# Small tiles of a decoder trunk padded and packed, so that the tiles behind them lie elsewhere in SBUF

## The chip, the cores and the metric

The kernel runs on one core of a Trainium2 chip. The metric is the device time of one execution in microseconds (us): the median of three runs is 1328.34 us, from 1328.08 to 1328.96. The profile is of one further execution.

## The reference

Two layers of a decoder trunk over 256 tokens of width 1024, all in float32. What matters of it here:

```python
for l in range(DEPTH):                                   # DEPTH = 2
    x = x + 0.5 * swiglu_ffn(x, ffn1_norm[l], ffn1_wi[l], ffn1_wo[l])      # 1024 -> 2 x 2816 -> 1024
    h = rms_norm(x, mix_norm[l])
    (sb_q, sb_k, sb_v, mla_cq, mla_ckv, mla_kr, nsa_q, ck, cv, sk, sv, wk, wv,
     nsa_gate, merge_gate) = jnp.split(h @ w_in[l], offsets, axis=-1)
    o_sb = stick_breaking_attention(...)                 # 8 heads of 64
    o_mla = mla_attention(...)                           # 8 heads, low-rank q and kv
    o_nsa = nsa_attention(..., nsa_gate, ...)            # 8 heads, three branches
    gates = jax.nn.sigmoid(merge_gate).reshape(B, S, 3, D_MODEL)
    y = (gates[:, :, 0] * (o_sb @ proj_sb[l]) + gates[:, :, 1] * (o_mla @ proj_mla[l])
         + gates[:, :, 2] * (o_nsa @ proj_nsa[l]))
    x = x + y @ w_out[l]
    x = x + 0.5 * swiglu_ffn(x, ffn2_norm[l], ffn2_wi[l], ffn2_wo[l])
```

## The kernel before, in words

**Products.** The tokens are two row tiles of 128 (`t` = 0, 1). Each float32 operand is split into a high part (rounded to float32r) and the low rest, and `mm3` (L528 to L532) makes three matmuls of a product: high by high (L530), high by the weights' low part (L531), low by the weights' high part (L532). The stationary operand is 128 x 128 of the activations, laid with the contracted dimension on the partitions: `hThi`, `hTlo` for the normed input, `gh`, `gl` for the inner activations of the FFN, `oh`, `ol` for the outputs of the attentions, `cT` for the latents of the MLA. The moving operand is the weights, `whi` and `wlo`, mostly 512 columns. The result goes to a PSUM bank `acc`.

**Weights.** They come from HBM in slabs of 128 x 1024 (`load_slab` in the FFNs, `weights` in the mixer): two DMAs into `raw`, then ScalarE rounds to `whi` (L514, L817) and VectorE subtracts to `wlo` (L515, L819). Four slabs are in the buffer.

**Stages of a layer.** `ffn`: first the products with `hT` in column chunks of 512 (`chunk`), where for a slab two steps of the contraction run into the same `acc` before the row tile changes; `glu` gates the result, and `flush` transposes it (L692) into `gh`, `gl`. Then `out_rows` multiplies `gT` by the 22 slabs of the output weights: for a slab it runs t = 0 and 1 and for each the column halves c = 0 and 1, three matmuls each, so that the bank changes after every three. That makes 264 matmuls in an `out_rows` of an FFN, in four of them (two layers with two FFNs). `mixer`: a planner (`Planner.run`) merges generators into one static order for TensorE, VectorE and ScalarE, by costs in a table; `t_chunk` (L849) is its loop for the products with weights, the same loop for the products with `hT` and for those of `merge` (L1147) with `oh`, `ol`. Behind the mixer `out_rows` runs the output projection with `hT`-like tiles.

**Order.** The order on TensorE, VectorE and ScalarE is fixed when the program is built. A tile's place in SBUF follows from the pools: a pool lays its tiles one behind another in each partition, and the pools stand behind each other (`cp`, `sm`, `wp`, `hp`, and then, in turn, `fp` of an FFN or `mp` of a mixer). A shift of one small tile in `hp` therefore shifts all of `fp` and `mp`.

Names that the change touches: `rn` (L572), the three scaled copies of a token's inverse norm; `krg0`, `krg1` (L875), the rotary key and gate logits of the MLA and NSA; `sg` (L1443), the gates of the NSA; `qrb` (L1022), the buffer of the query's rotation, with its one slot `s_qrb`; `new_oT` (L766, called in L1195), the tiles `oh` and `ol`; `wf` (L745), four work tiles with the slots `s_wf`.

Of the kernel before, what the change touches and what calls it, by code (L numbers as in the profile page):

```python
# [10 lines left out]
F = mybir.dt.float32  # L11
# [10 lines left out]
NT = 2  # L22
# [201 lines left out]
def event():  # L224
    return Tok(None)
# [78 lines left out]
def use_v(n, *deps, slots=()):  # L304

    return "V", 0.065 + 0.00106 * n, 0.15 + 0.00106 * n, deps, slots


def use_v1(n, *deps, slots=()):

    return "V", 0.13 + 0.00052 * n, 0.215 + 0.00052 * n, deps, slots


def use_a(n, *deps, slots=()):

    return "A", 0.085 + 0.00085 * n, 0.19 + 0.00085 * n, deps, slots
# [19 lines left out]
def use_g(us, *deps, slots=()):  # L336

    return "G", us, us, deps, slots
# [5 lines left out]
WR_BUFS = 4  # L344
TH_BUFS = 7
# [11 lines left out]
def decoder_trunk(ctx, tc, x_in, wts, gains, lcon, cst, out, depth=DEPTH):  # L357
# [7 lines left out]
    hp = ctx.enter_context(tc.tile_pool(name="hp", bufs=2))  # L365
# [10 lines left out]
    def att_tile():  # L376
        return pb.tile([128, 512], F, tag="ps", name="att")
# [156 lines left out]
    def rstd(ss, inv, w=1, p=128):  # L534
        r = sm.tile([128, 16], F, tag="rs", name="rs")
        nc.vector.tensor_scalar(ss[:p, :w], ss[:p, :w], inv, EPS, op0=OP.mult, op1=OP.add)  # L536
        nc.gpsimd.tensor_tensor(r[:p, :w], ss[:p, :w], mh[:p, :w], op=OP.pow)  # L537
        return r
# [25 lines left out]
    def norm_scale(t):  # L564

        sq = att_tile()
        ss = sm.tile([128, 16], F, tag="ss", name="ss")
        for c in range(2):
            nc.scalar.activation(sq, xs[t][:, c * 512:(c + 1) * 512], AF.Square, accum_out=ss[:, c:c + 1])
        nc.vector.tensor_scalar(ss[:, 0:1], ss[:, 0:1], ss[:, 1:2], None, op0=OP.add)  # L570
        r = rstd(ss, 1.0 / D)
        q = hp.tile([128, 3], F, tag="rn", name="rn", bufs=4)  # L572
        for i, m in enumerate((1.0, 0.5, 0.125)):
            nc.vector.tensor_scalar(q[:, i:i + 1], r[:, 0:1], m, None, op0=OP.mult)
        return q
# [28 lines left out]
    def out_rows(lhs, kts, between=None, last=False):  # L604
# [28 lines left out]
        for t in range(NT):  # L633
            cmajor = last or t == 0
            order = [(k, c) for k in tail for c in range(2)]
            if cmajor:
                order.sort(key=lambda kc: kc[1])
            for k, c in order:
                run(t, c, k, sls[k - tail[0]])
                if t == 1 and not last and c == 0 and k - tail[0] in (0, 1):  # L640
                    to_T(hT[0], hs[0], (k - tail[0],))
                if cmajor and k == kts - 1:
                    finish(t, c)
            if not cmajor:
                for c in range(2):
                    finish(t, c)
            if not last:
                rn[t] = norm_scale(t)
# [90 lines left out]
    def mixer(l):  # L739
        es = ExitStack()  # L740
        mp = es.enter_context(tc.tile_pool(name="mp", bufs=1))
        hs, hT, rn = nxt[0]
        xd = dp.tile([NT, 128, D], F, tag="xd", name="xd")

        def wf():  # L745
            return mp.tile([128, 384], F, tag="wf", name="wf", bufs=4)
# [7 lines left out]
        def tmp(n=768):  # L754
            return mp.tile([128, 768], F, tag="tmp", name="tmp", bufs=1)[:, :n]
# [10 lines left out]
        def new_oT():  # L766
            return (mp.tile([128, 4, S], R, tag="oh", name="oh", bufs=2),
                    mp.tile([128, 4, S], R, tag="ol", name="ol", bufs=2))
# [9 lines left out]
        s_bank = Slots(8)  # L778
        s_acc, s_tp, s_att = Slots(4, s_bank), Slots(2, s_bank), Slots(3, s_bank)
        s_w, s_raw = Slots(W_BUFS - len(ready)), Slots(RAW_BUFS)  # L780
        s_wf, s_wr, s_qk, s_th, s_tmp, s_qrb, s_of = Slots(4), Slots(WR_BUFS), Slots(4), Slots(TH_BUFS), Slots(1), Slots(1), Slots(1)

        def events(*n):
            return [events(*n[1:]) for _ in range(n[0])] if n else event()
# [87 lines left out]

        cT = mp.tile([128, 2, NT, 3, 128], R, tag="r3", name="cT")
        cT = cT[:, 0], cT[:, 1]
        krg = [mp.tile([128, 56], F, name=f"krg{t}") for t in range(NT)]  # L875
        ev_hT, ev_rn, ev_cT, ev_krg = events(2), [Tok(2.0), Tok(4.0)], events(NT), events(NT)

        def hT_rest():
# [93 lines left out]
        def mla_q(i):  # L972
            for t in range(NT):
                ks = []
                for c in range(2):
                    k = yield use_p(384, 6, ev_cT[t], slab_ev[i][c], slab_ev[i + 1][c], slots=(s_acc,))
                    a = acc_tile()
                    for s in range(2):
                        mm3(a[:, 0:384], cut(cT, A, t, s, A), cut(slabs[i + s][1], A, slice(c * 384, (c + 1) * 384)),
                            start=s == 0, stop=s == 1)  # L980
                    ks.append(event())
                    spawn(mla_q_out(t, c, a, k, ks[c]))
                spawn(mla_q_norm(t, ks), 0.4)
            s_w.put(k, k)
            mark()
            mark()
# [7 lines left out]
        def t_rope(dst, x, tb, t, H, d, buf, k):  # L994

            c, s = tb[0][:, t, :], tb[1][:, t, :]
            h = d // 2
            for o, i in ((0, h), (h, 0)):
                k1 = yield use_v(H * h, k)
                nc.vector.tensor_tensor(buf[:, :, o:o + h], x[:, :, i:i + h], bc(s[:, o:o + h], H), op=OP.mult)  # L1000
            k1 = yield use_v(H * d, k1)
            nc.vector.tensor_tensor(x, x, bc(c, H), op=OP.mult)
            k1 = yield use_v(H * d, k1)
            nc.vector.tensor_tensor(dst, x, buf, op=OP.add)
            return k1

        def mla_q_norm(t, ks):
            x = mq[t].rearrange("p (h d) -> p h d", h=8)
            k = yield use_a(768, *ks, slots=(s_tmp,))
            sq = tmp()  # L1010
            nc.scalar.activation(sq, mq[t], AF.Square)
            k = yield use_v(768, k)
            ss = sm.tile([128, 16], F, tag="ss", name="ss")
            nc.vector.tensor_reduce(ss[:, 0:8], sq.rearrange("p (h d) -> p h d", h=8), axis=AX.X, op=OP.add)
            s_tmp.put(k)
            k = yield use_v1(8, k)
            r = rstd(ss, 1.0 / 96, w=8)
            k = yield use_g(2.5, k)
            k = yield use_v(768, k)
            nc.vector.tensor_tensor(x, x, r[:, 0:8, None].to_broadcast([128, 8, 96]), op=OP.mult)  # L1020
            yield "-", 0.0, 0.0, (), (s_qrb,)
            b = mp.tile([128, 8, 32], F, tag="qrb", name="qrb", bufs=1)  # L1022
            k = yield from t_rope(x[:, :, 64:96], x[:, :, 64:96], tab["mq"], t, 8, 32, b, k)
            s_qrb.put(k)
            ev_mq[t].set(k)

        def mla_kv(i):
# [164 lines left out]
                yield from merge(c, *gs[c], o_nsa, ev_onsa, False, final=True)  # L1192


        o_sb, o_mla, o_nsa = new_oT(), new_oT(), new_oT()  # L1195
        ev_osb, ev_omla, ev_onsa = events(4), events(4), events(4)
        ev_sbpv, ev_sbm = event(), event()

# [241 lines left out]
                spawn(put_o(o_mla, p, oT, k, ev_omla), 0.01 * p)  # L1440


        sg = mp.tile([128, NT, 3, 8], F, name="sg")  # L1443
        ev_prep, ev_sg = events(NT), event()

        def nsa_prep():
# [381 lines left out]
```

## Time and profile before

| | |
|---|---|
| median of three runs | 1328.34 us |
| the profiled execution | 1328.05 us, its span 1326.3 us |
| TensorE (PE) busy | 1302.1 us, 98% of the span, 6623 matmuls |
| VectorE (DVE) busy | 893.9 us, 67% |
| ScalarE (ACT) busy | 796.4 us, 60% |
| share of the chain that ended last | PE 85%, ACT 7%, DVE 6%, issue 2% |
| mean granted clock of TensorE | 0.997 of 2.4 GHz |

The span is the time from the first to the last instruction; the execution is 1.75 us longer. A matmul's record is longer than the distance to the next one, since matmuls are pipelined: the pace of a stream is read from the starts of two records and the number of matmuls from the one to the other, not from a record's length. Where the text speaks of a record's length it says so.

### The profile page before, as it was taken

The numbers are of one execution on the slowest core, as the hardware profiler recorded it, in microseconds if no ns is written. First come the engines' busy times: TensorE is split into PE (matmuls) and PEld (weight loads), VectorE is DVE, ScalarE is ACT, GpSimd is POOL, SyncE is SP. The second block draws the span as 40 slices with busy tenths as digits, with TensorE's granted clock in tenths as the row PEclk, the third lists the DMA queues.
The fourth block names the chain that finished last, engine by engine and source line by source line (L and its number), as shares of the span: only waits on it lengthen the run. The fifth ranks groups of instructions, "written<-read, shape, count | busy, mean of one in ns | idle before, by whom it ended". The sixth has DMA issues, their size and how long they took to land.

```text
span 1326.3 us, 19987 instructions
## 1 busy us (share of the span) xinstructions
PE 1302.1 (98%) x6623; PEld 1078.1 (81%) x6623; DVE 893.9 (67%) x1852; ACT 796.4 (60%) x1654; POOL 43.4 (3%) x50
## 2 busy tenths in 40 slices
PE   7999999999899999999999999999989999999998
PEld 6888888888777888888888888888878778888887
DVE  6655557988997775555466554679879876755553
ACT  5545447796888555454464544478868884645442
POOL 0000000210000000000000000011100000000000
PEclk9999999999999999999999999999999999999999
DMA  7765557545434656555656565565453356565563
GB/s 226 245 190 177 189 179 219 181 127 175 128 90 135 184 174 198 189 183 183 191 179 216 178 190 181 188 217 160 133 173 110 102 159 176 173 191 183 183 189 112
DMA packets 124504, 230.77 MB, mean 174 GB/s; under 512 B 13928, under 2 KB 15600, under 8 KB 124400
## 3 DMA queue, kind: packets, MB, share of 16 engines
q1 hardware_dynamic: 124144, 228.97, 55.5%
q8 instruction: 52, 0.85, 0.3%
q0 software_dynamic: 256, 0.52, 0.1%
q14 instruction: 52, 0.43, 0.1%
HBM read 225.77 MB, written 3.15 MB: 173 GB/s over the span
## 4 chain that ended last, share of the span: by engine, by line
PE 85%; ACT 7%; DVE 6%; issue 2%; DMA 0%; SPq 0%; ACTq 0%; DVEq 0%
PE acc L530 26%; PE acc L532 26%; PE acc L531 26%; ACT wf L1340 2%; ACT whi L817 2%; PE tp L692 1%; DVE wlo L819 1%; ACT wf L1367 1%; DVE wr L1384 1%; DVE wlo L515 1%; DVE x L626 1%; PE att L1290 1%; PE att L1726 1%; PE att L1262 1%; DVE wf L1350 0%
## 5 line engine op out<-in xcount | busy, mean ns | idle before, releaser
L515 DVE TENSOR_TENSOR wlo<-raw,whi 128x512 fp32r<-128x512 f32 (+1 forms) x560 | 361.9, 687 | 318.0 <-ACT whi L514 316.6
L514 ACT ACTIVATE whi<-raw 128x512 fp32r<-128x512 f32 (+1 forms) x560 | 323.0, 623 | 374.7 <-PE acc L532 366.4
L530 PE MATMUL acc<-whi,hThi 128*128 128x512 f32 (+2 forms) x1248 | 480.3, 385 | 0.5 <-ACT hThi L525 0.5
L532 PE MATMUL acc<-whi,hTlo 128*128 128x512 f32 (+2 forms) x1248 | 470.4, 377 | 0.6 <-DVE hTlo L526 0.6
L531 PE MATMUL acc<-wlo,hThi 128*128 128x512 f32 (+2 forms) x1248 | 469.0, 376 | 0.0
L532 PEld LDWEIGHTS acc<-whi,hTlo 128*128 128x128 f32 x1248 | 235.3, 189 | 44.6 <-DVE hTlo L526 1.0
L530 PEld LDWEIGHTS acc<-whi,hThi 128*128 128x128 f32 x1248 | 235.7, 189 | 39.5 <-ACT hThi L525 1.0
L531 PEld LDWEIGHTS acc<-wlo,hThi 128*128 128x128 f32 x1248 | 235.9, 189 | 37.7
L819 DVE TENSOR_TENSOR wlo<-raw,whi 128x512 fp32r<-128x512 f32 (+1 forms) x276 | 181.4, 681 | 42.2 <-ACT whi L817 40.6
L817 ACT ACTIVATE whi<-raw 128x512 fp32r<-128x512 f32 (+1 forms) x276 | 162.9, 618 | 53.9 <-PE acc L532 42.4
L530 PE MATMUL acc<-whi,gh 128*128 128x512 f32 x352 | 140.1, 398 | 0.0
L532 PE MATMUL acc<-whi,gl 128*128 128x512 f32 x352 | 139.0, 395 | 0.0
L531 PE MATMUL acc<-wlo,gh 128*128 128x512 f32 x352 | 139.0, 395 | 0.0
L532 PEld LDWEIGHTS acc<-whi,gl 128*128 128x128 f32 x352 | 66.1, 188 | 15.9
L531 PEld LDWEIGHTS acc<-wlo,gh 128*128 128x128 f32 x352 | 66.2, 188 | 15.3
L530 PEld LDWEIGHTS acc<-whi,gh 128*128 128x128 f32 x352 | 66.1, 188 | 15.3
L537 POOL TENSOR_TENSOR rs<-ss,mh 128x1 f32<-128x1 f32 (+4 forms) x30 | 36.6, 1223 | 1034.0 <-DVE ss L536 1012.6
L1340 ACT ACTIVATE wf<-wf,mn 128x128 f32<-128x128 f32 x96 | 42.7, 446 | 12.1 <-DVE mn L1350 11.7
L530 PE MATMUL acc<-whi,oh 128*128 128x512 f32 x96 | 41.2, 429 | 0.5 <-DVE y L1155 0.5
L532 PE MATMUL acc<-whi,ol 128*128 128x512 f32 x96 | 39.1, 408 | 0.0
L531 PE MATMUL acc<-wlo,oh 128*128 128x512 f32 x96 | 39.1, 407 | 0.0
L683 DVE SCALAR_TENSOR_TENSOR g<-acc,rn,sil 128x512 f32<-128x512 f32 (+1 forms) x48 | 33.6, 703 | 2.9 <-PE acc L532 0.8
(274 smaller groups left out, 1262.6 us busy)
## 6 DMA issues: line engine op xcount, KB each, us to landing
raw<-in_wts SPq DMA_DIRECT2D x824, 256.0 KB, 2.7
gain<-in_gains SPq DMA_DIRECT2D x5, 512.0 KB, 5.7
xd<-x SPq DMA_DIRECT2D x4, 512.0 KB, 4.4
x<-xd SPq DMA_DIRECT2D x4, 512.0 KB, 4.1
raw<-in_wts SPq DMA_DIRECT2D x8, 184.0 KB, 2.5
lc<-in_lcon SPq DMA_DIRECT2D x2, 528.0 KB, 7.5
x<-in_x SPq DMA_DIRECT2D x4, 256.0 KB, 5.3
out_dram<-x SPq DMA_DIRECT2D x4, 256.0 KB, 2.0
```

Source lines behind the costliest of these rows:

```text
L514: nc.scalar.activation(hi[:, c:c + m], raw[:, :m], AF.Copy)
L515: nc.vector.tensor_tensor(lo[:, c:c + m], raw[:, :m], hi[:, c:c + m], op=OP.subtract)
L530: nc.tensor.matmul(o, a[0], b[0], start=start, stop=False)
L531: nc.tensor.matmul(o, a[0], b[1], start=False, stop=False)
L532: nc.tensor.matmul(o, a[1], b[0], start=False, stop=stop)
L537: nc.gpsimd.tensor_tensor(r[:p, :w], ss[:p, :w], mh[:p, :w], op=OP.pow)
L626: nc.vector.scalar_tensor_tensor(xv, accs[t, c], 0.5, xv, op0=OP.mult, op1=OP.add)
L683: nc.vector.scalar_tensor_tensor(g[:, :fn], b[:, :fn], rn[t][:, 0:1], s[:, :fn], op0=OP.mult, op1=OP.mult)
L692: nc.tensor.transpose(tp[:, j * 128:(j + 1) * 128], g[:, j * 128:(j + 1) * 128], ident)
L817: nc.scalar.activation(hl[0][:, c:c + m], raw[:, :m], AF.Copy)
L819: nc.vector.tensor_tensor(hl[1][:, c:c + m], raw[:, :m], hl[0][:, c:c + m], op=OP.subtract)
L1340: nc.scalar.activation(E[i][:, cs], E[i][:, cs], AF.Exp, scale=-1.0, bias=mn[:, q:q + 1], accum_out=su[:, q:q + 1])
```

## The change

The number of instructions, their order on all five engines and what they compute stay as they are (TensorE has 5930 rows in the order before and as many after, all alike but for line numbers and buffers' numbers). All semaphore waits stay too, except that two VectorE instructions wait for an earlier instruction of VectorE itself that stands three places before the one they waited for. What changes is where tiles lie. `rn` becomes 32 columns wide where it had 3; `krg0`, `krg1` and `sg` become parts of one tile `small` of 1024 bytes a partition; `qrb` goes, and the rotation takes one of the four `wf` tiles for it; and the six tiles of `new_oT` and `small` are allocated ahead of the tiles behind them.

Start of each tile in a partition, modulo 512 bytes, as the built programs have it (all slices of 128 columns and of 512 columns that the products with weights take lie whole multiples of 512 bytes further, except the second half of a slab of 440 columns, which lies 224 more):

| tile | before | after |
|---|---|---|
| `whi`, `wlo`, `raw`, `hThi`, `hTlo` | 32 | 32 |
| `gh`, `gl`, `sil`, `g` (FFN) | 160 | 32 |
| `oh`, `ol` (outputs of the attentions) | 96 | 32 |
| `cT`, `zw`, `V0`, `V1` | 160 | 32 |
| `nx0`, `nx1` | 96 | 32 |
| `Vc`, `pch`, `pcl`, `wf`, `th`, `qk`, `wr`, `of`, `tmp` | 288 | 32 |
| `rt`, `zk`, `hv` and `ident` (constants) | 352, 352 or 96, 352 or 96, 320 | unchanged |

```diff
@@ -569,7 +569,7 @@
             nc.scalar.activation(sq, xs[t][:, c * 512:(c + 1) * 512], AF.Square, accum_out=ss[:, c:c + 1])
         nc.vector.tensor_scalar(ss[:, 0:1], ss[:, 0:1], ss[:, 1:2], None, op0=OP.add)
         r = rstd(ss, 1.0 / D)
-        q = hp.tile([128, 3], F, tag="rn", name="rn", bufs=4)
+        q = hp.tile([128, 32], F, tag="rn", name="rn", bufs=4)
         for i, m in enumerate((1.0, 0.5, 0.125)):
             nc.vector.tensor_scalar(q[:, i:i + 1], r[:, 0:1], m, None, op0=OP.mult)
         return q
@@ -778,7 +778,7 @@
         s_bank = Slots(8)
         s_acc, s_tp, s_att = Slots(4, s_bank), Slots(2, s_bank), Slots(3, s_bank)
         s_w, s_raw = Slots(W_BUFS - len(ready)), Slots(RAW_BUFS)
-        s_wf, s_wr, s_qk, s_th, s_tmp, s_qrb, s_of = Slots(4), Slots(WR_BUFS), Slots(4), Slots(TH_BUFS), Slots(1), Slots(1), Slots(1)
+        s_wf, s_wr, s_qk, s_th, s_tmp, s_of = Slots(4), Slots(WR_BUFS), Slots(4), Slots(TH_BUFS), Slots(1), Slots(1)
 
         def events(*n):
             return [events(*n[1:]) for _ in range(n[0])] if n else event()
@@ -872,7 +872,9 @@
 
         cT = mp.tile([128, 2, NT, 3, 128], R, tag="r3", name="cT")
         cT = cT[:, 0], cT[:, 1]
-        krg = [mp.tile([128, 56], F, name=f"krg{t}") for t in range(NT)]
+        o_sb, o_mla, o_nsa = new_oT(), new_oT(), new_oT()
+        small = mp.tile([128, 256], F, name="small")
+        krg = [small[:, 56 * t:56 * t + 56] for t in range(NT)]
         ev_hT, ev_rn, ev_cT, ev_krg = events(2), [Tok(2.0), Tok(4.0)], events(NT), events(NT)
 
         def hT_rest():
@@ -1018,10 +1020,10 @@
             k = yield use_g(2.5, k)
             k = yield use_v(768, k)
             nc.vector.tensor_tensor(x, x, r[:, 0:8, None].to_broadcast([128, 8, 96]), op=OP.mult)
-            yield "-", 0.0, 0.0, (), (s_qrb,)
-            b = mp.tile([128, 8, 32], F, tag="qrb", name="qrb", bufs=1)
+            yield "-", 0.0, 0.0, (), (s_wf,)
+            b = wf()[:, 0:256].rearrange("p (h d) -> p h d", h=8)
             k = yield from t_rope(x[:, :, 64:96], x[:, :, 64:96], tab["mq"], t, 8, 32, b, k)
-            s_qrb.put(k)
+            s_wf.put(k)
             ev_mq[t].set(k)
 
         def mla_kv(i):
@@ -1192,7 +1194,6 @@
                 yield from merge(c, *gs[c], o_nsa, ev_onsa, False, final=True)
 
 
-        o_sb, o_mla, o_nsa = new_oT(), new_oT(), new_oT()
         ev_osb, ev_omla, ev_onsa = events(4), events(4), events(4)
         ev_sbpv, ev_sbm = event(), event()
 
@@ -1440,7 +1441,7 @@
                 spawn(put_o(o_mla, p, oT, k, ev_omla), 0.01 * p)
 
 
-        sg = mp.tile([128, NT, 3, 8], F, name="sg")
+        sg = small[:, 112:160].rearrange("p (t b h) -> p t b h", t=NT, b=3)
         ev_prep, ev_sg = events(NT), event()
 
         def nsa_prep():
```

## Rows read from the trace of the kernel before

**Rows 1.** The page: busy time of the engines, and the chain of work that ended last, by engine and by line.

```profile
PE 1302.1 (98%) x6623; PEld 1078.1 (81%) x6623; DVE 893.9 (67%) x1852; ACT 796.4 (60%) x1654; POOL 43.4 (3%) x50
...
PE 85%; ACT 7%; DVE 6%; issue 2%; DMA 0%; SPq 0%; ACTq 0%; DVEq 0%
PE acc L530 26%; PE acc L532 26%; PE acc L531 26%; ACT wf L1340 2%; ACT whi L817 2%; PE tp L692 1%; DVE wlo L819 1%; ACT wf L1367 1%; DVE wr L1384 1%; DVE wlo L515 1%; DVE x L626 1%; PE att L1290 1%; PE att L1726 1%; PE att L1262 1%; DVE wf L1350 0%
```

**Rows 2.** Busy time by stretch (us from the span's start: PE, weight loads, DVE, ACT and POOL with their instructions, then the granted clock, the DMA share and GB/s): an `out_rows` of an FFN, the chunks of the next FFN, a merge with `oh`, the products with `hT` behind it, and a stretch of the mixer with waits.

```profile
137.00:197.00 60.00, 60.00 (x264) 48.42 (x263) 30.64 (x48) 24.67 (x44) 0.00 (x0) 1.00 0.56 180
552.00:572.00 20.00, 20.00 (x93) 16.52 (x93) 11.56 (x20) 9.90 (x18) 0.00 (x0) 1.00 0.58 188
616.00:662.00 46.00, 46.00 (x201) 37.07 (x199) 22.69 (x35) 19.62 (x35) 0.00 (x0) 1.00 0.61 186
308.00:313.00 5.00, 5.00 (x24) 4.05 (x23) 4.96 (x10) 2.67 (x5) 0.00 (x0) 1.00 0.70 235
314.00:324.00 10.00, 10.00 (x45) 8.26 (x44) 8.33 (x17) 5.38 (x10) 0.00 (x0) 1.00 0.71 205
328.00:340.00 12.00, 8.62 (x38) 6.19 (x35) 9.63 (x30) 9.88 (x29) 0.00 (x0) 0.86 0.37 111
```

**Rows 3.** The groups of large products over the whole span, by form (count, busy us, mean length of a record in ns, idle time before).

```profile
L531 PE MATMUL acc<-wlo,hThi 128*128 128x512 f32 x1056 | 411.7, 390 | 0.0
...
L531 PE MATMUL acc<-wlo,gh 128*128 128x512 f32 x352 | 139.0, 395 | 0.0
...
L531 PE MATMUL acc<-wlo,oh 128*128 128x512 f32 x96 | 39.1, 407 | 0.0
...
L532 PE MATMUL acc<-whi,cT 128*128 128x384 f32 x16 | 5.4, 338 | 0.0
```

**Rows 4.** The timeline of TensorE, start in us first: the products with `hT` of the second FFN's chunks, a run of 84 matmuls without another instruction between them (first two rows, both counted), and out of a steady stretch of such a run three rows, of which the last is the eighth matmul behind the first.

```profile
567.63 0.48 PE L530 MATMUL acc<-whi,hThi 128*128 128x512 f32 x1
...
586.58 0.39 PE L532 MATMUL acc<-whi,hTlo 128*128 128x512 f32 x1
...
559.98 0.39 PE L530 MATMUL acc<-whi,hThi 128*128 128x512 f32 x1
560.21 0.39 PE L531 MATMUL acc<-wlo,hThi 128*128 128x512 f32 x1
...
561.79 0.39 PE L532 MATMUL acc<-whi,hTlo 128*128 128x512 f32 x1
```

**Rows 5.** The timeline of TensorE in `out_rows` of the same FFN: the run of `gh` and `gl` from 616.09 to 662.82, 201 matmuls from the first row to the last, both counted, nothing between them; and two rows behind each other out of another stretch of it.

```profile
616.09 0.47 PE L530 MATMUL acc<-whi,gh 128*128 128x512 f32 x1
...
662.82 0.39 PE L532 MATMUL acc<-whi,gl 128*128 128x512 f32 x1
...
640.66 0.39 PE L530 MATMUL acc<-whi,gh 128*128 128x512 f32 x1
640.89 0.40 PE L531 MATMUL acc<-wlo,gh 128*128 128x512 f32 x1
```

**Rows 6.** The timeline of TensorE in the mixer: a merge of `oh` and `ol` (24 matmuls from 307.96 to 313.33, both counted) and, right behind it, products with `hT` by the same loop (48 matmuls from 313.56 to 324.23).

```profile
307.96 0.40 PE L530 MATMUL acc<-whi,oh 128*128 128x512 f32 x1
...
313.33 0.40 PE L532 MATMUL acc<-whi,ol 128*128 128x512 f32 x1
313.56 0.39 PE L530 MATMUL acc<-whi,hThi 128*128 128x512 f32 x1
...
324.23 0.39 PE L532 MATMUL acc<-whi,hTlo 128*128 128x512 f32 x1
```

**Rows 7.** The timeline of TensorE at the start of the mixer: the last 15 products of 440 columns, from the first row here to the second, which is the next product, of 512 columns.

```profile
208.92 0.36 PE L530 MATMUL acc<-whi,hThi 128*128 128x440 f32 x1
...
211.93 0.39 PE L530 MATMUL acc<-whi,hThi 128*128 128x512 f32 x1
```

**Rows 8.** Who TensorE waited for in the whole span (us in total, times, longest), and two rows of the mixer's timeline with the idle time before them.

```profile
PE tp L1376 <- ACT wf L1367: 9.0, 10, 2.4
PE tp L412 <- DMA ident<-in_cst: 3.3, 1, 3.3
PE tp L550 <- DMA x<-in_x: 3.2, 2, 2.2
...
333.74 0.33 PE L1376 MATMUL tp<-ident,wf 128*128 128x128 f32 x1 [2.36 <-ACT wf L1367]
334.86 0.44 PE L1376 MATMUL tp<-ident,wf 128*128 128x128 f32 x2 [0.79 <-ACT wf L1367]
```

**Rows 9.** Products of the attentions whose operands move, by form over the whole span (count, busy us, mean length of a record in ns, idle time before).

```profile
L1290 PE MATMUL att<-wr,rt 128*128 128x384 f32 x32 | 10.8, 391 | 0.0
L1222 PE MATMUL acc<-wr,V 128*128 128x256 f32 x32 | 10.5, 327 | 0.0
...
L1743 PE MATMUL acc<-wr,V 128*128 128x512 f32 x16 | 7.0, 439 | 0.1
```

**Rows 10.** The splits of one shape into tiles at two places, by tile: what ScalarE and VectorE take for 128x512 from PSUM (ns min/median/max).

```profile
L525 ACT ACTIVATE gh<-tp x48: 362/582/584, 31.3 to 1272.8; 128x512 fp32r<-128x512 f32 x40, 128x256 fp32r<-128x256 f32 x8
L526 DVE TENSOR_TENSOR gl<-tp,gh x48: 418/684/685, 32.1 to 1273.7; 128x512 fp32r<-128x512 f32 x40, 128x256 fp32r<-128x256 f32 x8
...
L525 ACT ACTIVATE hThi<-tp x20: 579/589/602, 197.7 to 1139.3; 128x512 fp32r<-128x512 f32 x20
L526 DVE TENSOR_TENSOR hTlo<-tp,hThi x20: 682/690/693, 198.3 to 1140.0; 128x512 fp32r<-128x512 f32 x20
```

## The prediction, made before the changed kernel was run

> **What bounds the kernel now.** I read the page first. TensorE is busy for 98% of the span and has 85% of the chain that ended last; 78% of the span are the three lines of `mm3` [rows 1]. The waits of TensorE come next: 6.5 us go to two DMAs at the start, about 9 us to ten waits for the probabilities in the mixers, and little else is above a microsecond [rows 8]. Then the stretches: in `out_rows` of an FFN TensorE is busy all the time at the full clock, while VectorE and ScalarE are busy for about half of it and the DMAs for 0.56 to 0.61 [rows 2]. So in the FFNs, and in most of the mixer, the time is the number of matmuls times their pace; a nanosecond saved on each is saved on the clock. Nothing is queued in front of TensorE that could take its place: the products with `hT` draw on the same slabs, at 188 GB/s [rows 2], and run faster.
>
> How fast, the timeline tells. The run of 84 products with `hT` takes 18.95 us from first to last start, 228.3 ns each; once it has settled, eight steps take 1.81 us, 226 ns [rows 4]. The 48 in the mixer take 10.67 us over 47 steps, 227.0 ns [rows 6]. The run of 201 products with `gh` and `gl` takes 46.73 us over 200 steps: 233.65 ns [rows 5]. The 24 of the merge, with `oh` and `ol`, take 5.37 us over 23 steps: 233.5 ns [rows 6]. All have 128 x 128 stationary and 512 moving columns at 2.4 GHz, the weights at 32 modulo 512. What differs is where the stationary tile lies: `hT` at 32 as the weights, `gh` at 160, `oh` at 96. The whole gap is 6.5 to 6.65 ns a matmul, and it doesn't grow with the distance.
>
> Two things speak for the place and against the loop as the cause. The merge and the `hT` products behind it run through the same loop, `t_chunk`, one right after the other, and the pace changes from 233.5 to 227.0 with the tile alone [rows 6]. And the products of 440 columns use `hT`, but the second half of their slab lies 224 bytes off: 15 of them take 3.01 us, 200.7 ns each [rows 7]. At 2.4 GHz 440 columns stream in 183.3 ns; with what an aligned product adds to its columns (227.0 less 213.3, 13.7) they would take 197.0. They take 3.7 more, about half of 6.65, as when one in two is slow. A pair at equal places therefore costs its columns and some 13 ns, any other some 20.
>
> **The change part by part.**
>
> *FFN, output product.* Four `out_rows` of 264 matmuls each, 1056 in all [rows 2, 3], go from 160 to 32. Upper bound: 233.65 less 227.0 is 6.65 ns, times 264 is 1.76 us, times four 7.0. Lower bound: with the pace of the run that begins behind transposes, 228.3, it is 5.35 ns, 1.41 us, 5.6 in all. Such a run pays its start once, 83 steps of 1.3 ns or 0.11 us, and an `out_rows` has two `flush`es, so 1.76 less 0.2: I take 1.6 us each, **6.4 us**. It is all on the path: TensorE has no gap there.
>
> *Mixer, merges.* 3 x 96 = 288 matmuls with `oh`, `ol` [rows 3] go from 96 to 32. Upper bound: 6.5 ns each, 1.9 us. Lower bound nothing: the merges are cut up by attention matmuls, a run needs its start anew each time, and where TensorE waits for probabilities anyway, as between 331 and 335 us [rows 8], what it gains becomes a longer wait. I take two thirds, **1.2 us**, nearer to the row of the long merge.
>
> *Mixer, latents.* 16 products in each of three lines with 384 columns [rows 3] and 24 in all with 512, from 160 to 32: 72 at 6.5 ns at most are 0.5 us, at least none; **0.2 us**.
>
> *Attention products.* Scores have both operands at the same place before and after. `wr` against `V` goes from 288 and 160 to 32 and 32, a gain if anything; `wr` against `rt` from 288 and 352 to 32 and 352, unequal as before. Their largest groups are 28.3 us busy [rows 9]; the gap of 6.65 in 233.65, 2.8%, is 0.8 us on them, either way. I take nothing.
>
> *Transposes, padding, packing.* The transposes' moving operand is `ident` at 320, unequal to all before and after: nothing. `rn` with 32 columns is still read one column at a time; `krg` and `sg` in one tile, and `wf` in place of `qrb`, leave order and waits as they are: nothing. The planner's slots could have moved work, but the order shows that they didn't.
>
> *VectorE and ScalarE on moved tiles.* No row shows an operation at two places in one stage. The nearest: splits into `gh`, `gl` (160) take 582 and 684 ns, into `hT` (32) 589 and 690 [rows 10], 1.2% and 0.9% more. On all of the chain's ACT and DVE, 7% and 6% of 1326.3 us or 93 and 80 us, that would be 1.1 and 0.7, a loss of 1.8 us at most; most of the chain's pieces there (splits of weights) don't move, and I take nothing.
>
> Sum: 6.4 + 1.2 + 0.2 = 7.8 us. From the profiled execution, 1328.05, that leaves 1320.25; its span goes from 1326.3 to 1318.5, with 1.75 around it as before. The median of the runs was 0.3 us above the profiled one, so **1320.5 us**. The bounds together: at most 7.0 + 1.9 + 0.5 + 0.8 = 10.2, 1318.1; at least 5.6 less 0.8 less 1.8 = 3.0, 1325.3.
>
> **The rivals.**
>
> *The loop is the cause in `out_rows`.* There the bank changes every three matmuls, in `chunk` every six; the slow pace of `gh` could be that. Then only merges and latents gain, 1.4 us: 1326.9. Against it: the merge keeps its bank as `hT` does and has the pace of `out_rows` to 0.15 ns [rows 5, 6].
>
> *The place plays no part at all.* What reads as an effect of the place would be one of the tile's shape or of the stage, and nothing changes: 1328.3. For it: the rows only compare different tiles, never one tile at two places. Against it: the products of 440 columns, where tile and stage are one [rows 7].
> The Trainium skill has a rule that speaks for this rival: "TensorE: Matmul & The Clock Gate", section "Step-by-step: what each phase is for", gives TensorE two independent read ports, one for the streaming operand and one for the weight load, so where the two lie should not matter. By that rule the time stays; the trace doesn't bear it out, with 227.0 against 233.5 ns in one loop [rows 6].
>
> *The shared place costs the other engines.* With nearly every tile at 32, reads and writes of VectorE and ScalarE in the mixer could meet TensorE's more often, in the softmax chains (`wf`, `wr`) that TensorE waits for [rows 8]. It decides from 4.5%: the chain's 173 us of ACT and DVE times 0.045 is 7.8. At 10% it would be 17.3 less 7.8: slower by 9.5, 1337.8. Against it: the splits of weights, raw to `whi` to `wlo` all at 32, run beside `hT` at 32 without slowing TensorE [rows 2, 4], and the splits at either place differ by about 1% [rows 10].
>
> **How the numbers follow.** The forecast has 0.82, the loop 0.07, no part 0.07, the slower one 0.04. A measurement of this kernel tells about 0.2%, 2.7 us, from no change. The forecast, down to its weakest bound, is faster by more than that (1325.3 against 1325.7): faster 0.82. Loop and no part fall within it: same 0.14. Slower 0.04. The range goes from 1317.5, a little under the upper bound of the gain, to 1324.5: it leaves out the three rivals and the weakest corner of the forecast, not quite 2 in 10.
>
> **What would show it.** In the profile after, the run of 201 products with `gh` and `gl` should take about 45.5 us, and the records of L531 with `gh`, 395 ns on average, should come down to the 389 or 390 of `hThi` [rows 3]; the 24 of the merge should take some 5.23 to 5.3 us; `hT` should stay. If `gh` stays at 233 and `oh` falls, it was the loop; if both stay, the place plays no part. If both fall and the time doesn't, the gain was lost in waits: the idle time of TensorE before L1376, 9.0 us, would have grown. One thing could take more than that wait: behind it the granted clock is 0.86 on average over 12 us, which is 3.4 us at 1.2 GHz [rows 2]; another such drop would cost 1.7 us. And ScalarE's and VectorE's records on moved tiles should keep their length within 1%.

## The result, and the profile after

The changed kernel takes 1320.27 us (median of six runs, 1319.62 to 1321.55) against 1328.59 us of the kernel before in the same series (1327.98 to 1329.28): a ratio of 0.9938, 95% interval 0.9926 to 0.9951. That is 0.6% faster, 0.2 us from the forecast and inside its range. The profiled execution took 1320.05 us.

The page after: the span, the busy time of the engines and the chain that ended last, which answer to [rows 1].

```profile
span 1318.3 us, 19987 instructions
...
PE 1294.1 (98%) x6623; PEld 1078.1 (82%) x6623; DVE 893.3 (68%) x1852; ACT 796.4 (60%) x1654; POOL 43.3 (3%) x50
...
PE 84%; ACT 7%; DVE 6%; issue 2%; DMA 0%; SPq 0%; DVEq 0%; ACTq 0%
```

The span is 8.0 us shorter, and TensorE's busy time fell by exactly 8.0 (1302.1 to 1294.1) with the same 6623 matmuls. VectorE and ScalarE are where they were, within 0.6 us. The same work runs faster on the engine that was the bound, and that engine is still the bound.

The timeline of TensorE after (start in us first): the merge of 24 and the 48 products with `hT` behind it, the run of 84 with `hT`, and the run of 201 with `gh` and `gl`; they answer to [rows 6], [rows 4] and [rows 5].

```profile
305.82 0.40 PE L530 MATMUL acc<-whi,oh 128*128 128x512 f32 x1
...
311.06 0.39 PE L532 MATMUL acc<-whi,ol 128*128 128x512 f32 x1
311.29 0.39 PE L530 MATMUL acc<-whi,hThi 128*128 128x512 f32 x1
...
321.94 0.39 PE L532 MATMUL acc<-whi,hTlo 128*128 128x512 f32 x1
...
565.09 0.48 PE L530 MATMUL acc<-whi,hThi 128*128 128x512 f32 x1
...
584.04 0.39 PE L532 MATMUL acc<-whi,hTlo 128*128 128x512 f32 x1
...
613.25 0.48 PE L530 MATMUL acc<-whi,gh 128*128 128x512 f32 x1
...
658.72 0.39 PE L532 MATMUL acc<-whi,gl 128*128 128x512 f32 x1
```

The 201 take 45.47 us over 200 steps, 227.35 ns each, where they took 233.65. The 24 of the merge take 5.24 us (227.8 ns) where they took 5.37. The runs with `hT`, whose tiles didn't move, take 10.65 and 18.95 us against 10.67 and 18.95. So of these runs only those whose stationary tile moved changed their pace.

The groups of products after, by form (count, busy us, mean length of a record in ns, idle time before); [rows 3] has them before.

```profile
L531 PE MATMUL acc<-wlo,hThi 128*128 128x512 f32 x1056 | 411.5, 390 | 0.0
...
L531 PE MATMUL acc<-wlo,gh 128*128 128x512 f32 x352 | 136.9, 389 | 0.0
...
L531 PE MATMUL acc<-wlo,oh 128*128 128x512 f32 x96 | 38.6, 402 | 0.0
```

The record of `gh` fell from 395 to 389, within 1 ns of that of `hThi`.

Where the 8 us came from, by the starts of the same matmul in both traces: the four `out_rows` of the FFNs became 1.55, 1.55, 1.55 and 1.63 us shorter (63.06 to 61.51 in the first three, 62.21 to 60.57 in the last), 6.28 in all; the two mixers 249.46 to 249.02 and 249.63 to 249.11, 0.96 in all. Some 0.8 are left, which no term had foreseen: 0.3 at the start, most of it inputs that landed earlier, and the rest in small pieces elsewhere. Both traces have two stretches at 1.2 GHz of about 3.4 us, one behind the wait of either mixer, so the clock has little part in these differences.

Who TensorE waited for, the row that answers to the first of [rows 8]: the wait did not grow.

```profile
PE tp L1377 <- ACT wf L1368: 9.0, 10, 2.4
```

### The profile page after: what moved, and what is told of

Its sections match the earlier page's. It is cut to its first block, busy times and chain, and to the rows that moved or that the text cites. A ratio compares the mean times of both kernels' runs of the same rounds, so it can differ in the third digit from the quotient of the medians.

```text
span 1318.3 us, 19987 instructions
## 1 busy us (share of the span) xinstructions
PE 1294.1 (98%) x6623; PEld 1078.1 (82%) x6623; DVE 893.3 (68%) x1852; ACT 796.4 (60%) x1654; POOL 43.3 (3%) x50
## 4 chain that ended last, share of the span: by engine, by line
PE 84%; ACT 7%; DVE 6%; issue 2%; DMA 0%; SPq 0%; DVEq 0%; ACTq 0%
PE acc L530 26%; PE acc L532 26%; PE acc L531 26%; ACT wf L1341 2%; ACT whi L817 2%; PE tp L692 1%; DVE wlo L819 1%; ACT wf L1368 1%; DVE wr L1385 1%; DVE wlo L515 1%; DVE x L626 1%; PE att L1291 1%; PE att L1727 1%; DVE wf L1351 1%; PE tp L1377 1%
## 5 line engine op out<-in xcount | busy, mean ns | idle before, releaser
L530 PE MATMUL acc<-whi,hThi 128*128 128x512 f32 (+2 forms) x1248 | 480.2, 385 | 0.5 <-ACT hThi L525 0.5
L532 PE MATMUL acc<-whi,hTlo 128*128 128x512 f32 (+2 forms) x1248 | 470.1, 377 | 0.4 <-DVE hTlo L526 0.4
L531 PE MATMUL acc<-wlo,hThi 128*128 128x512 f32 (+2 forms) x1248 | 469.0, 376 | 0.0
L532 PEld LDWEIGHTS acc<-whi,hTlo 128*128 128x128 f32 x1248 | 235.4, 189 | 44.1 <-DVE hTlo L526 0.9
L530 PEld LDWEIGHTS acc<-whi,hThi 128*128 128x128 f32 x1248 | 235.8, 189 | 39.2 <-ACT hThi L525 1.0
L531 PEld LDWEIGHTS acc<-wlo,hThi 128*128 128x128 f32 x1248 | 236.1, 189 | 37.6
L530 PE MATMUL acc<-whi,gh 128*128 128x512 f32 x352 | 138.3, 393 | 0.0
L532 PE MATMUL acc<-whi,gl 128*128 128x512 f32 x352 | 137.1, 390 | 0.0
L531 PE MATMUL acc<-wlo,gh 128*128 128x512 f32 x352 | 136.9, 389 | 0.0
L532 PEld LDWEIGHTS acc<-whi,gl 128*128 128x128 f32 x352 | 66.1, 188 | 13.9
L531 PEld LDWEIGHTS acc<-wlo,gh 128*128 128x128 f32 x352 | 66.1, 188 | 13.4
L530 PEld LDWEIGHTS acc<-whi,gh 128*128 128x128 f32 x352 | 66.1, 188 | 13.2
L530 PE MATMUL acc<-whi,oh 128*128 128x512 f32 x96 | 41.3, 430 | 0.5 <-DVE y L1157 0.5
L531 PE MATMUL acc<-wlo,oh 128*128 128x512 f32 x96 | 38.6, 402 | 0.0
L532 PE MATMUL acc<-whi,ol 128*128 128x512 f32 x96 | 38.5, 401 | 0.0
```

Source lines behind the costliest of these rows:

```text
L530: nc.tensor.matmul(o, a[0], b[0], start=start, stop=False)
L531: nc.tensor.matmul(o, a[0], b[1], start=False, stop=False)
L532: nc.tensor.matmul(o, a[1], b[0], start=False, stop=stop)
```

## The experiments

All are the changed kernel with tiles moved by padding, so the order of the instructions is the same unless said otherwise. Where a line is added, `mm3` stands at L531 to L533 or further down. "At 160" means 160 bytes into a block of 512, as in the table of the change; the distance between a stationary tile and the weights is what follows from it.

**1. Only the FFN's tiles stay moved.** The mixer's tiles go back off the weights, to 96.

```diff
+        mp.tile([128, 16], F, name="mpad")
         Vs = [mp.tile([128, NT, 8, 2, 64], R, name=f"V{i}") for i in range(2)]
```

> The changed kernel with 64 bytes ahead of all tiles of the mixer: gh and gl stay at 32, while oh, ol, cT, wr, V, wf and the rest of the mixer go to 96. Theory (a stationary tile at another place modulo 512 than the weights costs some 6.6 ns a matmul): the FFN's gain of 6.4 us stays and the mixer's 1.4 goes, 1321.7 us; 24 products of the merge in 5.37 us, 201 of gh in 45.5 us. Rival (the gain is not local to the products whose tiles are aligned): the merge keeps 5.24 us and the time 1320.3.

Measured: 1321.73 us (1320.93 to 1323.68), ratio 0.9947 [0.9935, 0.996]. The merge is back at its old pace, 23 steps in 5.37 us, while the run of 201 with `gh` keeps 45.46 us:

```profile
305.83 0.40 PE L530 MATMUL acc<-whi,oh 128*128 128x512 f32 x1
...
311.20 0.40 PE L532 MATMUL acc<-whi,ol 128*128 128x512 f32 x1
...
613.57 0.48 PE L530 MATMUL acc<-whi,gh 128*128 128x512 f32 x1
...
659.03 0.39 PE L532 MATMUL acc<-whi,gl 128*128 128x512 f32 x1
```

The FFN half of the change carries most of the gain. The rival in which the loop is the cause falls: `out_rows` changes its bank as before and is fast.

**2. Only the mixer's tiles stay moved.** `rn` is narrow again, which puts the FFN's tiles back to 160, and a pad holds the mixer's at 32.

```diff
-        q = hp.tile([128, 32], F, tag="rn", name="rn", bufs=4)
+        q = hp.tile([128, 3], F, tag="rn", name="rn", bufs=4)
...
+        mp.tile([128, 96], F, name="mpad")
         Vs = [mp.tile([128, NT, 8, 2, 64], R, name=f"V{i}") for i in range(2)]
```

> The changed kernel with rn 3 columns wide again, and 384 bytes ahead of the tiles of the mixer instead: gh and gl go back to 160, the mixer's tiles stay at 32. Theory: the FFN's 6.4 us go, 1326.8 us; 201 products of gh in 46.73 us, 24 of the merge in 5.24 us. Rival (alignment of the FFN's tiles matters through something else than these products): gh stays at 45.5 us.

Measured: 1328.53 us (1326.9 to 1329.43), ratio 0.9994 [0.9985, 1.0003], no difference from before that can be told. In its trace the merge takes 5.24 us, as after, and the run with `gh` is back at 233.7 ns. So the merges are faster in the trace, and hardly any of it reaches the end. Two things blur it. The first is seen in windows over the mixer's wait (columns as in [rows 2]). In experiment 1, second layer:

```profile
980.00:1000.00 20.00, 16.67 (x88) 13.22 (x85) 15.94 (x50) 15.51 (x47) 0.61 (x1) 0.83 0.33 98
```

In experiment 2, first and second layer:

```profile
325.00:345.00 20.00, 16.46 (x122) 13.78 (x121) 15.33 (x49) 16.69 (x47) 0.28 (x1) 1.00 0.43 133
980.00:1000.00 20.00, 16.59 (x111) 13.73 (x110) 14.75 (x44) 15.43 (x43) 0.00 (x0) 0.91 0.43 143
```

Behind the wait for the probabilities the granted clock is 0.83 on average in one execution, 0.91 in another place and 1.00 in a third. By estimate, at 1.2 GHz half the speed is lost, so 0.91 over 20 us means 3.6 us at the low level and 1.8 us lost, 0.83 twice that, 1.00 nothing. Executions of one kernel differ by that step (the mean granted clock of the eleven here goes from 0.996 to 0.999), so a term of about 1 us in the mixer is at the edge of what such runs can tell.

The clock alone does not hide the gain, though: the execution of this trace has one stretch at 1.2 GHz fewer in its mixers than that of before, and is still 0.48 us longer. Its start took 0.95 us more (27 matmuls between 11 and 17 us, where the trace of before has 36). And in the second mixer a slab of weights landed late, so that ScalarE and then TensorE waited where TensorE waits for nothing before and after:

```profile
871.98 0.94 ACT L818 ACTIVATE whi<-raw 128x512 fp32r<-128x512 f32 x2 [1.84 <-DMA raw<-in_wts]
...
874.34 0.52 PE L918 MATMUL tp<-ident,wf 128*128 128x128 f32 x3 [1.19 <-DVE wf L911]
```

Among the executions with a mean granted clock of 0.997, eight of this kernel have a median of 1327.99 us and twelve of the kernel before 1329.12, 1.1 us apart. The group was picked out afterwards, so this is a hint that the term is there, and no proof.

**3. The stationary tiles away from the weights, all of them.** A pad of 128 bytes ahead of everything in `hp` puts `hT`, `gh`, `oh` and the rest of the mixer at 160.

```diff
+    hp.tile([128, 32], F, tag="pad", name="pad", bufs=1)
     xs = []
```

> The changed kernel with 128 bytes ahead of x: hT, gh, gl, oh, ol, cT and all of the mixer lie at 160, weights and raw at 32. Theory: all large products are slow, 3168 with hT, 1056 with gh and 288 with oh, 4512 in all at 6.65 ns or 30.0 us, and 480 of 256 columns at the same price or none, 0 to 3.2 us: 1350 to 1354 us. The run of 84 products with hT takes 19.4 us. Rival (only gh and oh are sensitive, for their shapes or their stages): 1328.

Measured: 1341.21 us (1340.55 to 1341.63), ratio 1.009 [1.0076, 1.0103]: 20.9 us over the changed kernel and slower than before, as the place would have it, but some 10 us less than expected. One and the same kind of product, with `hT` in the chunks, now stands at two places in two kernels. A run of 84 here:

```profile
55.88 0.47 PE L531 MATMUL acc<-whi,hThi 128*128 128x512 f32 x1
...
75.32 0.40 PE L533 MATMUL acc<-whi,hTlo 128*128 128x512 f32 x1
```

It takes 19.44 us where such a run takes 18.95 after: 234.2 against 228.3 ns. The rival in which the place plays no part falls with this: the tile, the loop and the stage are the same. The size was missed at `hT`: against the trace after, its 3168 products of 512 columns lose 14.3 us, 4.5 ns each and not 6.65, while those of `gh` and `gl` lose 6.3 us as in the kernel before and the merges 0.7. A run of `hT` pays a start when it is aligned (228.3 over the run, 226.67 once settled) and less of one when it isn't (234.2, 233.4), so this run loses 5.9 ns a product. The runs of 84 lose 5.3 on average, since most of them settle at 232.5 here, and the short runs of the mixer, of 3 to 12 products, lose 1.3 to 3.4. Why the same distance gives 233.4 in some runs and 232.5 in others is open. And narrower products lose less or nothing: the median step of `hT`'s 256 columns is 120 ns after and 119 here, of the 440 columns 200 and 202.

**4. Weights and stationary tiles moved together.** The same pad stands ahead of the weights, so that all lie at 160.

```diff
+    cp.tile([128, 32], F, name="pad")
     mh = cp.tile([128, 16], F, name="mh")
```

> The changed kernel with 128 bytes ahead of weights and all that stands behind them: weights, raw, hT, gh, oh and the mixer's tiles all at 160, constants where they were. Theory (what counts is that both operands lie alike): 1320.3 us, hT 226.7 ns, gh 227.3 ns. Rival (a stationary tile has to lie at 32 for its own sake, or weights have to): hT, gh and oh all slow, 1350 us.

Measured: 1320.89 us (1320.42 to 1323.4), ratio 0.9943 [0.993, 0.9955], the time of the changed kernel. A run of 84 with `hT` and the run of 201 with `gh`:

```profile
56.26 0.48 PE L531 MATMUL acc<-whi,hThi 128*128 128x512 f32 x1
...
75.20 0.39 PE L533 MATMUL acc<-whi,hTlo 128*128 128x512 f32 x1
...
615.32 0.48 PE L531 MATMUL acc<-whi,gh 128*128 128x512 f32 x1
...
660.78 0.39 PE L533 MATMUL acc<-whi,gl 128*128 128x512 f32 x1
```

They take 18.94 and 45.46 us: `hT` settles at 226.67 ns, `gh` runs at 227.3. It is the place of one operand relative to the other that counts, not either place itself.

**5. Only `hTlo` away.** 128 bytes stand between `hThi` and `hTlo`, so that one product in three (L532) is unequal; `rn` becomes narrower by as much, and all that follows stays at 32.

```diff
+        hp.tile([128, 32], F, tag="pad", name="pad", bufs=1)
...
-        q = hp.tile([128, 32], F, tag="rn", name="rn", bufs=4)
+        q = hp.tile([128, 24], F, tag="rn", name="rn", bufs=4)
```

> The changed kernel with 128 bytes between hThi and hTlo, and what follows kept at 32: hThi at 32, hTlo at 160. Of the three matmuls of a product L530 and L531 have hThi, L532 has hTlo. Theory A (a running stream meets the load of the next stationary tile): the step from L531 to L532 is slow and the other two are quick, up to 1056 times 6.65 or 7.0 us more, 1327. Theory B (a stream meets its own stationary tile): the step from L532 to the next L530 is slow, the same time. Rival (a stretch of products is slow as a whole once one place differs): all three slow, as with all of hT moved, some 16 us more, 1336.

Measured: 1331.92 us (1330.33 to 1333.36), ratio 1.0021 [1.0009, 1.0032], between the two expected times. The groups of a run of `hT`, between 58 and 76 us:

```profile
L530 PE MATMUL acc<-whi,hThi 128*128 128x512 f32 x26 | 10.1, 389 | 0.0
L531 PE MATMUL acc<-wlo,hThi 128*128 128x512 f32 x27 | 10.7, 396 | 0.0
L532 PE MATMUL acc<-whi,hTlo 128*128 128x512 f32 x26 | 10.3, 397 | 0.0
```

Two of three have the long record, though only L532 has an unequal pair of its own. From start to start, in settled runs, the steps are 226.7 (behind L530), 232.5 (behind L531) and 234.1 (behind L532): the product whose stationary tile is off is slow, and so is the one ahead of it. One slow step in three is wrong, then, and so are three.

**6, 7 and 9. Other distances.** Pads put `hT`, `gh` and `oh` at 256, 32 and 192 bytes from the weights (sixth), at 32, 16 and 256 (seventh), and at 192, 224 and 96 (ninth).

```diff
+    hp.tile([128, 64], F, tag="pad", name="pad", bufs=1)
...
-        q = hp.tile([128, 32], F, tag="rn", name="rn", bufs=4)
+        q = hp.tile([128, 16], F, tag="rn", name="rn", bufs=4)
...
+            fp.tile([128, 8], F, tag="fpad", name="fpad", bufs=1)
...
+        mp.tile([128, 112], F, name="mpad")
```

The diff is that of the sixth; the seventh and the ninth have other widths at the same places (the seventh lays `gh` and `gl` 16 bytes into a wider tile).

> The changed kernel with hT 256 bytes off the weights, gh and gl 32 bytes off, oh, ol and the mixer's tiles 64 bytes before them. Theory (512 is the modulus and any distance costs the same): as with all stationary tiles 128 off, hT 233.3, gh 233.7, oh 233.3 ns, 1341 us. Rival 1 (the modulus is 256): hT stays at 226.7 to 228.3 ns and the time is 1328. Rival 2 (a distance of 32 is too small to matter, or the cost goes by the distance): gh between 227.3 and 233.

> The changed kernel with hT 32 bytes off the weights, gh and gl 16 bytes off, oh, ol and the mixer's tiles 256 bytes off. Theory (any distance costs the same): hT 233.3, gh 233.7, oh 233.3 ns, 1341 us. Rival (small distances cost little): hT and gh at 227 to 230 ns, 1321 to 1330 us; with oh at 256 quick if the modulus is 256.

> The changed kernel with hT 192 bytes behind the weights, that is 64 before them modulo 256, gh and gl 224 behind, oh, ol and the mixer's tiles 96 behind. Theory (the modulus is 256 and the direction counts, as the merge 64 before the weights showed with 228.9 ns): hT 228.9 ns once settled, gh between 227 and 233, oh 233.3; 1330 to 1336 us. Rival (that merge was an accident of short runs, any distance costs the same): hT, gh, oh all at 233.3 to 233.7 ns, 1341 us.

Measured: 1327.33 us (ratio 0.9988 [0.9978, 0.9998]), 1342.27 us (1.0098 [1.0079, 1.0116]) and 1332.85 us (1.0028 [1.0016, 1.0039]). The sixth gave the rival with a modulus of 256 and not the theory; the seventh and the ninth gave the times of theirs. In the timelines, a run of 84 with `hT` at a distance of 256 (sixth):

```profile
55.71 0.48 PE L531 MATMUL acc<-whi,hThi 128*128 128x512 f32 x1
...
74.66 0.39 PE L533 MATMUL acc<-whi,hTlo 128*128 128x512 f32 x1
```

the run of 201 with `gh` at 16 and a merge with `oh` at 256 (seventh):

```profile
152.72 0.48 PE L531 MATMUL acc<-whi,gh 128*128 128x512 f32 x1
...
199.47 0.40 PE L533 MATMUL acc<-whi,gl 128*128 128x512 f32 x1
...
312.00 0.40 PE L531 MATMUL acc<-whi,oh 128*128 128x512 f32 x1
...
317.22 0.40 PE L533 MATMUL acc<-whi,ol 128*128 128x512 f32 x1
```

and `hT` at 192 (ninth):

```profile
79.00 0.47 PE L531 MATMUL acc<-whi,hThi 128*128 128x512 f32 x1
...
98.08 0.39 PE L533 MATMUL acc<-whi,hTlo 128*128 128x512 f32 x1
```

At 256 the 84 take 18.95 us and the 24 take 5.22: as quick as at 0. At 16 the 201 take 46.75 us: as slow as at 128. The paces of settled runs over all kernels, by the distance between stationary tile and weights:

| distance in bytes | ns a product of 512 columns |
|---|---|
| 0 and 256 | 226.67 |
| 16, 32, 64, 96, 128 and 224 | 233.3 (234 for the merges at 96, 232.5 in most runs of `hT` at 128) |
| 192 (also as -64) | 228.9 |

So the place counts modulo 256, not 512, and it is nearly all or nothing: 16 bytes off cost as much as 128, and only 192 is a middle case, with a mean a third of the way up. None of the tiles that the table of the change pairs with the weights (`gh` at 128 bytes from them, `oh` at 64, `cT` at 128) differed by just 256, so this kernel gains nothing from the wider rule.

**8. Everything else aligned too.** The constants (`ident`, and `rt`, `zk` in the mixer) are brought to the place of the weights, and a slab of 440 columns is laid so that its second half starts 512 columns in, no longer 224 bytes off (it is then loaded and split in two pieces of 440 columns, not of 512 and 368).

```diff
+    g_col = cp.tile([128, 8], F, name="g_col")
...
-    g_col = cp.tile([128, 8], F, name="g_col")
...
+    cp.tile([128, 80], F, name="pad")
     mh = cp.tile([128, 16], F, name="mh")
...
-                    mm3(a[:, :440], cut(hT[t], A, k, A), cut(slabs[i][1], A, slice((k % 2) * 440, (k % 2 + 1) * 440)),
+                    mm3(a[:, :440], cut(hT[t], A, k, A), cut(slabs[i][1], A, slice((k % 2) * 512, (k % 2) * 512 + 440)),
```

> The changed kernel with the constants brought in line too: ident, rt, zk, weights, hT, gh, oh and the mixer's tiles all at 352, and the second half of a slab of 440 columns moved to a whole multiple of 512 bytes. Theory (the price is paid by large products alone, a transpose's pace of 108 to 109 ns is set by something else): 96 products of 440 columns gain 3.7 ns each, 0.35 us, and the rest stays, 1319.9 us, transposes still 108 to 109 ns apart. Rival (transposes pay it too): some 560 transposes gain up to 6.65 ns each, 3.7 us, 1316.2.

Measured: 1323.47 us (1322.53 to 1326.15), ratio 0.9962 [0.9947, 0.9977]: no gain over the changed kernel. The last 18 products of 440 columns here, up to the next of 512:

```profile
207.24 0.36 PE L536 MATMUL acc<-whi,hThi 128*128 128x440 f32 x1
...
210.84 0.40 PE L536 MATMUL acc<-whi,hThi 128*128 128x512 f32 x1
```

3.60 us over 18 are 200.0 ns each, and the changed kernel, with its second half 224 bytes off, has the same:

```profile
206.98 0.36 PE L530 MATMUL acc<-whi,hThi 128*128 128x440 f32 x1
...
209.98 0.39 PE L530 MATMUL acc<-whi,hThi 128*128 128x512 f32 x1
```

3.00 us over 15. These products are not slowed by lying 224 bytes off. The transposes did not gain either: their records (of `g`, with `ident`) are 271 ns long against 272 after. VectorE's order differs a little in this kernel, and its mixers are 1.3 to 1.8 us longer; in the first, the stretch at 1.2 GHz is also twice as long as after. Which of these costs what is not told apart.

**10. The two parts of the weights apart.** 128 bytes between `whi` and `wlo`; the stationary tiles stay equal to `whi` modulo 256.

```diff
+    hp.tile([128, 32], F, tag="pad", name="pad", bufs=1)
...
-        return wp.tile([128, 1024], R, tag="whi", name="whi"), wp.tile([128, 1024], R, tag="wlo", name="wlo")
+        hi = wp.tile([128, 1024], R, tag="whi", name="whi")
+        wp.tile([128, 32], F, tag="pad3", name="pad3", bufs=1)
+        return hi, wp.tile([128, 1024], R, tag="wlo", name="wlo")
```

> The changed kernel with wlo and raw 128 bytes off whi, and hT, gh, oh and the mixer 256 bytes off whi, which counts as the same place: the streams of L530 and L532 lie as the stationary tiles, the stream of L531 doesn't. Theory A (a step is slow when the running stream lies otherwise than the tile that it uses or the next one): only the step from L531 to L532 is slow, 1504 products at 6.65 ns or 10.0 us more, 1330. Theory B (a step is slow whenever the distance between stream and stationary tile changes or differs on either side of it): the steps from L530 to L531 and from L531 to L532 are slow, 231.1 ns on average, up to 20 us more with less for starts, 1336 to 1340. Rival: all three slow, 1341.

Measured: 1340.56 us, ratio 1.0085 [1.0066, 1.0103]. The groups of a run of `hT`, 58 to 76 us:

```profile
L533 PE MATMUL acc<-whi,hThi 128*128 128x512 f32 x26 | 10.3, 397 | 0.0
L534 PE MATMUL acc<-wlo,hThi 128*128 128x512 f32 x26 | 10.3, 395 | 0.0
L535 PE MATMUL acc<-whi,hTlo 128*128 128x512 f32 x26 | 10.2, 392 | 0.0
```

Only L534 has an unequal pair, and all three are long; the steps behind them are 235.6, 233.8 and 230.2 ns. Theory A, which gave 1330, falls. By theory B the step behind L535 would be quick, and it is half slow; the time is nearest to the rival's, with all three slow. One unequal product in three slows two or three of them, so the price does not hang on a product's own pair alone. Which access meets which stays open: no simple rule (own pair, or own pair and the next stationary tile) gives both this and experiment 5.

**11. The constants alone.** Experiment 8 without its change to the slabs.

```diff
+    g_col = cp.tile([128, 8], F, name="g_col")
...
-    g_col = cp.tile([128, 8], F, name="g_col")
...
+    cp.tile([128, 80], F, name="pad")
     mh = cp.tile([128, 16], F, name="mh")
```

> The changed kernel with the constants alone brought in line, ident, rt, zk and all else at 352, and the slabs of 440 columns as they were. Theory (ident's place doesn't matter, and the loss of the run with the slabs rearranged came from the planner's other order and from the clock): 1320.3 to 1320.9 us, transposes 108 to 109 ns apart. Rival (constants in line cost the mixer something): mixer 1 us longer in each layer, 1322.5.

Measured: 1323.0 us (1320.33 to 1324.3), ratio 0.9955 [0.9942, 0.9969]. Its profiled execution took 1320.33 us, with mixers of 249.25 and 249.07 us against 249.02 and 249.11 after. The place of the constants neither helps nor harms in the trace; that the median lies 2.7 us higher, nearer to the rival's 1322.5, isn't explained by it. The four other executions have a mean granted clock of 0.996 where the profiled one has 0.997, so part of it goes with the clock. No version ran faster than the changed kernel.

## Why the prediction was right

*What bounds the kernel.* TensorE's pace of matmul, with its place as the cause: shown. Experiment 3 slows `hT` by moving it, with all that is laid behind it, away from the weights; 5 slows its products by moving `hTlo` alone; 4 moves both operands and keeps the pace; 1 keeps the loop of `out_rows` and its gain. What in the chip makes the place count is not shown. The Trainium skill gives TensorE independent read ports for the streaming operand and for the weight load ("TensorE: Matmul & The Clock Gate", section "Step-by-step: what each phase is for"). That the place should not matter, as the prediction drew from it, is not borne out here: one tile, `hT`, runs at 226.67 ns at the place of the weights and at 232.5 to 233.4 ns 128 bytes from it.

*FFN, output product.* 6.4 us forecast, 6.28 measured, 1.55 to 1.63 an `out_rows` where 1.6 was taken.

*Mixer, merges and latents.* 1.2 and 0.2 us forecast; the mixers became 0.96 us shorter. Without the tenth at either end, the mean step of the 260 steps between neighbouring merge products fell by 3.6 ns (237.2 to 233.6), which over 288 products is 1.0 us, a little more than half of the 6.5 ns of the long merge: the merges are cut up, as the term's lower bound had it. In the two profiled executions, whose clock dropped alike, it reaches the end of the mixers. How much of it the medians show is not settled: experiment 2 alone gains 0.3 us (1328.53 against 1328.82 beside it), experiment 1 misses 1.5 (1321.73 against 1320.27), and both are within the scatter.

*The sum.* That the forecast came within 0.2 us is in part luck. The terms were 0.6 us too large together (7.8 against 6.28 and 0.96), and the 0.8 us that no term had foreseen made up for it.

*Latents by themselves.* With 512 columns the median step went from 232 to 227 ns, with 384 from 175 to 173; the term took 6.5 for both. At 384 columns the price of the place is about a third.

*Attention products, transposes.* Forecast at nothing. The transposes of `g` keep records of 272 ns, and the largest attention groups stay within 3 ns a record of [rows 9]:

```profile
L1291 PE MATMUL att<-wr,rt 128*128 128x384 f32 x32 | 10.8, 391 | 0.0
L1223 PE MATMUL acc<-wr,V 128*128 128x256 f32 x32 | 10.4, 325 | 0.0
...
L1744 PE MATMUL acc<-wr,V 128*128 128x512 f32 x16 | 7.0, 436 | 0.1
```

*VectorE and ScalarE.* Forecast at nothing, with a loss of 1.8 us as the bound. The splits that [rows 10] showed, now at the weights' place (ns min/median/max):

```profile
L525 ACT ACTIVATE gh<-tp x48: 362/580/582, 31.0 to 1266.2; 128x512 fp32r<-128x512 f32 x40, 128x256 fp32r<-128x256 f32 x8
L526 DVE TENSOR_TENSOR gl<-tp,gh x48: 418/684/686, 31.8 to 1267.0; 128x512 fp32r<-128x512 f32 x40, 128x256 fp32r<-128x256 f32 x8
```

580 for 582 and 684 for 684: sharing a place costs these engines nothing here, and the rival that made the kernel slower falls. The 1% that [rows 10] showed between `gh` and `hT` is not the place's.

*A step of the argument that was wrong without harm.* The prediction took the products of 440 columns for a control within one tile: 200.7 ns as the mean of one slow half and one quick half [rows 7]. Experiment 8 aligns the second half and the pace stays 200.0. So 3.0 of the 3.7 ns over its 197.0 belong to the number of columns, so "columns and some 13 ns" was not a law; nor is "any other place costs 20": the price depends on the columns, and it is modulo 256 with a middle case at 192. What carried the forecast was the other comparison, 233.5 to 227.0 in one loop [rows 6].

*The clock.* The drop behind the mixer's wait was named as the one thing that could take more than the wait, at 1.7 us. It is there after as before; how long it lasts varies between executions, from nothing to twice that (experiments 1 and 2).

## What to carry to other kernels

Where a stream of float32r matmuls with a weight load each sets the time, compare its pace between starts across the tiles that it uses; a gap of 3% between equal shapes on a full clock is worth a look at where the stationary and the moving tile lie. In this kernel equal offsets modulo 256 bytes made 512-column products cheapest, a pad of some columns in a small tile was all it took, and moving both operands together changed nothing. A control inside one trace is only one if everything but the suspected cause is equal, and a different number of columns is not.

## What the runs showed of the hardware that was not expected

The period is 256 bytes, not 512 (18.95 us for 84 products at 256 as at 0), and 192 bytes costs 228.9 ns, a third of the full price. The paces of aligned products are 120.0 ns for 256 columns, about 173 for 384 (in short runs alone), 200.0 for 440 and 226.67 for 512; at 2.4 GHz that is 288, some 416, 480 and 544 periods, 32 more than the columns if 440 is counted as 448. The slow 233.3 ns are 560, 16 more. The price is for the wide products: with 256 columns the median step of `hT` is 120 ns aligned, 119 at 128 and 117 at 32 bytes off. And one unequal product slows its neighbours (experiments 5 and 10), by a mechanism that these runs leave open.
